# FFN down projection of a diffusion layer: two of the four weight sums of a chunk formed by accumulating transfers, the second output half carried negated

## The chip, the cores and the metric

The kernel runs on one core of one Trainium2 chip. The metric is the device time of one execution in microseconds (us). A core has TensorE (PE in the profile, its weight loads PEld), VectorE (DVE), ScalarE (ACT), GpSimd (POOL) and SyncE (SP), each with an instruction queue of its own that it works through in order, and 16 DMA engines that carry out the transfers these queues issue.

## What is computed

One layer of a hybrid model for 640 tokens (512 latent, 128 context) of 2048 channels: a modulated norm, one input projection, two groups of heads (gated DeltaNet and latent attention), an output projection with a gated residual, then a second modulated norm and a gated convolutional FFN, again with a gated residual, and a final norm. The change lies in the last product of the FFN:

```
def conv_ffn(h, w_up, conv_w, conv_b, w_down):
    u = depthwise_conv_centred(h @ w_up, conv_w) + conv_b
    a, gate = jnp.split(u, 2, axis=-1)
    return (jax.nn.silu(a) * gate) @ w_down

x = x + gate2 * conv_ffn(h2, w_up, ffn_conv_w, ffn_conv_b, w_down)
y = rms_norm(x, final_norm_g)
```

`w_down` is 5632 x 2048 in float32. Products are exact to near float32: each operand is split into a high and a low part, and three of the four part products are summed.

## The kernel before, in words

The tokens lie in the columns (640), the channels in the 128 partitions. Both FFN products are computed by halves of output channels, contraction and tokens, with 7 products in the place of 8 (Strassen's scheme in Winograd's form). For a pair of output tiles (256 channels) with weight quarters A11, A12 (first output half, first and second half of the contraction) and A21, A22 (second output half), the weights' side needs A11, A12, A22 and four sums:

```
S1 = A21 + A22     S2 = S1 - A11     S3 = A11 - A21     S4 = A12 - S2
```

**FFN down, order of the work.** The contraction is cut into 11 groups n, the output into 8 pairs p. A weight chunk (n, p) is 128 x 4 x 256, 512 KB: two contraction tiles of each half. `blocks`, `order` and `units` (lines 1478 to 1481) list the work: block 0 is four chunks by plain products (unit W); blocks 1 to 8 have eight chunks each (four pairs by two groups), block 9 twelve, block 10 eight. Each of these 84 chunks is two units: R (A11, S3, A12, A22; 24 matmuls of 128x128 by 320 columns) and S (S1, S4, S2; 18 matmuls).

**The loop** over the units (from line 1781) does, for unit u: `d_prep(u + 1)`, `d_mm(u)`, `d_post(u - 1)`, the residual of a finished pair, one step of the operands made ahead (`g_steps`).

- `d_load(i)` (L1524, DMA at L1527) loads chunk i on SP's queue into a `wraw` buffer, of which there are two; it is called for i + 2 when the R weights of chunk i have been split.
- `d_sums(i)` (L1529) forms the four sums on POOL: S1 at L1535 into a buffer `us` or `vs` (by the parity of i, one of each), the three differences by `sub` (its instruction stands at L1267); S3 takes the place of A21 inside `wraw`. It is called when the S weights of the chunk before have been split. Each is an instruction of 128 x 256.
- `d_prep(u)` splits the weights of a unit into `whi` by ACT (L922) and `wlo` by DVE (L923), two buffers of each; so it runs one unit ahead of the matmuls.
- `d_mm(u)` (L1594 high parts, L1597 low parts) accumulates in PSUM, tiles `mm` for R and `dn` for S.
- `d_post(u, q)` at a pair's last group adds the products to the output, which lies in SBUF (`xw`, `x_hi`, `x_lo`): ACT copies two products into `x` and `y` (L1622, L1623, one buffer of each), DVE adds what is read from PSUM, and POOL does three additions of 128 x 320 between SBUF tiles (L1601 is the helper `add` of both engines).
- `g_prep(j)` (L1512, instructions at L1517) makes the operands' sums: four subtractions of 128 x 320 on POOL for each of a group's two tiles, then splits by ACT and DVE.
- `residual2` (from line 1653), in the blocks 9 and 10: squares on ACT (L1666), added on POOL (L1668).

The program builder takes these instructions in the order in which they are written, but may move one ahead of another on the same engine where nothing depends on it. Waits between engines are put in by it.

Of the kernel before, what the change touches and what calls it, by code (L numbers as in the profile page):

```python
# [54 lines left out]
def _order():  # L55
    """the output tiles of the input projection"""
# [11 lines left out]
def step_kernel(ctx: ExitStack, tc: tile.TileContext, a, dbg=None, stop=None):  # L68
# [38 lines left out]
    # ------------------------------------------------------------ the stream of weight chunks  # L107
# [31 lines left out]
    def w_next():  # L139
        """the parts of the next chunk; the one after it is split and two more are loading."""  # L140
        i = pos[0]
        pos[0] += 1
        w_split(i)
        w_split(i + 1)
        w_load(i + 2)
        w_load(i + 3)
        raws_.pop(i, None)
        return parts.pop(i)

    # ------------------------------------------------------------ background work  # L150
# [7 lines left out]
    def fill_tick(n=1.0):  # L158
        """the filler advances by one unit every fill["step"] ticks."""
# [21 lines left out]
    # ------------------------------------------------------------ products  # L181
    def mm3(ps_list, wts, k, col, movs, start, stop):
        """ps += w^T m over the exact parts: hi.hi + hi.lo + lo.hi."""
# [9 lines left out]
    def hi_pass(outs, wts, col, mov, start, ticks=True):  # L193
        """outs = or += w_hi^T (m_hi + m_lo) over 4 k tiles."""
# [8 lines left out]
    def lo_pass(outs, wts, col, mov, stop, ticks=True):  # L203
        """outs += w_lo^T m_hi over 4 k tiles."""
# [13 lines left out]
    def dense(movs, sink, ntile=2, before=None, alloc=None, ext=0):  # L218
        """ntile output tiles, contraction over 16 tiles of 128."""
# [27 lines left out]
    # ------------------------------------------------------------ conditioning  # L247
# [9 lines left out]
    def ada(n, t0, cond, pl):  # L257
        """tiles t0 and t0 + 1 of the modulation; the last step is left to the caller"""
# [19 lines left out]
    def gain(t0, vg, n):  # L278
        """mod[scale] <- g * (1 + scale) for n channel tiles."""
# [4 lines left out]
    def modulated(x, rb, hi, lo, kt, scale, v):  # L284
        """(hi, lo) <- x * rb * gs; columns 0:512 by c, the rest by c_ctx."""
# [6 lines left out]
    def gemv_fill(pl, jobs):  # L292
        """vectors times matrices of up to 512 columns, in steps; a job: the weights of a k tile, the columns,
        the vectors [P, k, 2], and what becomes of the sums [P, (tile, c)]."""
# [47 lines left out]
    def ada_jobs(t0, t1):  # L342
        """four tiles of the modulation at a time"""
# [10 lines left out]
    # ------------------------------------------------------------ first norm, modulation, input projection  # L354
# [3 lines left out]
    # the normed and scaled tokens, and the two shifts as further columns  # L358
# [8 lines left out]
    with tc.tile_pool(name="xp", bufs=1, side="right") as xp:  # L367
# [25 lines left out]
        def early(i, ps):  # L393
            """z of a head, without the shift's part"""
# [45 lines left out]
    # ------------------------------------------------------------ gated DeltaNet  # L440
# [1472 lines left out]
```

## Time and profile before

| | us |
|---|---|
| median of 3 runs | 3420.69 (3416.08 to 3429.83) |
| span of the profiled execution | 3419.2 |
| PE busy in it | 3136.4 (92%) |
| DVE busy | 2657.2 (78%) |
| ACT busy | 1445.7 (42%) |
| POOL busy | 1584.5 (46%) |
| FFN down, from the first R unit's matmuls to the last S unit's | about 2778 to 3391 |

The span is that of one profiled execution, from the first instruction to the last; the median is that of the runs, 1.5 us more. The busy shares are averages over stages that differ: the slices of the page and the table by stretch show each stage by itself. In a group's row stand the line, the engine, the operation, what it writes and reads, the shape and the count; behind the bar the busy time, the mean of one in ns, and the idle time of the engine just before, with what ended it. Weight quarters and their sums have the names of their buffers: `wraw`, `us`, `vs`.

### The profile page before, as it was taken

How to read it: one execution, taken by the hardware profiler on the slowest of the kernel's cores; microseconds unless marked ns; L12 is line 12 of the kernel's file. 1: busy time of each engine (PE TensorE's matmuls, PEld its weight loads, DVE VectorE, ACT ScalarE, POOL GpSimd, SP SyncE). 2: the span in 40 equal slices, each digit the busy share in tenths (PEclk: the TensorE clock that was granted, in tenths of full speed). 3: DMA queues.
4: the chain of work that ended last, by engine and by line, in shares of the span. 5: the costliest groups of instructions: out<-in, count | busy, mean ns of one | idle time of the engine just before them, and what ended most of it. 6: DMA issues, size and time to landing. Idle time of an engine off the chain costs nothing.

```text
span 3419.2 us, 54842 instructions
## 1 busy us (share of the span) xinstructions
PE 3136.4 (92%) x21243; PEld 3017.4 (88%) x21243; DVE 2657.2 (78%) x3954; ACT 1445.7 (42%) x2230; POOL 1584.5 (46%) x1128
## 2 busy tenths in 40 slices
PE   5889999999999989997899999999999989988896
PEld 4689989889888979997799899999999988888895
DVE  7765666867576759998978887987888778787877
ACT  5434554554545542116344344344334444333433
POOL 1211111111100002326466566566566589999986
PEclk9998999998999999998899999999999999999998
DMA  7652222323242227772333433333332233232323
GB/s 268 215 169 64 81 81 72 102 67 97 65 140 73 78 69 274 268 240 86 123 102 98 126 109 101 117 104 102 119 109 95 97 118 101 88 99 90 104 99 116
DMA packets 181477, 403.94 MB, mean 118 GB/s; under 512 B 39392, under 2 KB 57952, under 8 KB 181216
## 3 DMA queue, kind: packets, MB, share of 16 engines
q1 hardware_dynamic: 181216, 400.44, 36.3%
q8 instruction: 167, 2.74, 0.3%
q14 instruction: 94, 0.77, 0.1%
HBM read 361.83 MB, written 38.54 MB: 117 GB/s over the span
## 4 chain that ended last, share of the span: by engine, by line
PE 55%; DVE 18%; POOL 11%; issue 6%; DMA 5%; ACT 4%; SPq 0%; DVEq 0%; POOLq 0%; ACTq 0%
PE mm L198 17%; PE mm L207 9%; PE dn L198 7%; DVE aacc L326 4%; PE dn L207 4%; DMA araw<-in_w_ada_dram 3%; PE mm L1594 3%; DVE wlo L923 2%; POOL wraw L1267 2%; PE pj L188 2%; DVE L L640 1%; DVE wlo L131 1%; PE mm L1083 1%; DVE tm L638 1%; POOL us L1267 1%
## 5 line engine op out<-in xcount | busy, mean ns | idle before, releaser
L131 POOL TENSOR_TENSOR wlo<-wraw,whi 128x1024 fp32r<-128x1024 f32 x61 | 189.6, 3109 | 986.6 <-PE mm L207 462.3
L923 DVE TENSOR_TENSOR wlo<-wraw,whi 128x1024 fp32r<-128x1024 f32 x256 | 402.5, 1572 | 162.5 <-ACT whi L922 82.8
L922 ACT CAST whi<-wraw 128x1024 fp32r<-128x1024 f32 x256 | 267.9, 1047 | 463.1 <-PE dn L198 159.7
L326 DVE SCALAR_TENSOR_TENSOR aacc<-araw,csil,aacc 128x512 f32<-128x512 f32 x510 | 421.1, 871 | 20.8 <-DMA araw<-in_w_ada_dram 19.8
L198 PE MATMUL mm<-b_hi,whi 128*128 128x320 f32 x1344 | 404.0, 314 | 11.3 <-ACT whi L922 10.5
L198 PE MATMUL mm<-b_lo,whi 128*128 128x320 f32 x1344 | 402.0, 313 | 0.0
L198 PE MATMUL mm<-h_hi,whi 128*128 128x320 f32 (+1 forms) x1312 | 330.5, 331 | 9.1 <-ACT h_hi L289 6.7
L198 PE MATMUL mm<-h_lo,whi 128*128 128x320 f32 (+1 forms) x1312 | 320.6, 324 | 12.3 <-POOL h_lo L290 12.3
L198 PE MATMUL dn<-b_hi,whi 128*128 128x320 f32 x1008 | 298.3, 310 | 1.0 <-ACT whi L922 1.0
L198 PE MATMUL dn<-b_lo,whi 128*128 128x320 f32 x1008 | 298.2, 309 | 0.0
L1594 PE MATMUL mm<-b_hi,whi 128*128 128x320 f32 x672 | 216.1, 335 | 67.6 <-DVE x_lo L1601 21.4
L198 PEld LDWEIGHTS mm<-b_hi,whi 128*128 128x128 f32 x1344 | 257.7, 192 | 13.4 <-ACT whi L922 12.3
L1294 POOL TENSOR_TENSOR us<-wraw,wraw 128x512 f32<-128x512 f32 x83 | 138.9, 1674 | 275.8 <-DVE wlo L923 275.8
L207 PE MATMUL mm<-b_hi,wlo 128*128 128x320 f32 x1344 | 234.2, 318 | 27.6 <-DVE wlo L923 27.5
L129 ACT CAST whi<-wraw 128x1024 fp32r<-128x1024 f32 (+1 forms) x138 | 142.8, 1035 | 273.9 <-PE mm L198 189.1
L198 PEld LDWEIGHTS mm<-b_lo,whi 128*128 128x128 f32 x1344 | 257.2, 191 | 0.0
L1267 POOL TENSOR_TENSOR wraw<-wraw 128x512 f32<-128x512 f32 (+1 forms) x168 | 247.6, 1474 | 13.1
L198 PEld LDWEIGHTS mm<-h_lo,whi 128*128 128x128 f32 x1312 | 230.9, 197 | 16.1 <-POOL h_lo L290 14.2
L198 PEld LDWEIGHTS mm<-h_hi,whi 128*128 128x128 f32 x1312 | 230.1, 198 | 15.1 <-ACT h_hi L289 8.7
L207 PEld LDWEIGHTS mm<-b_hi,wlo 128*128 128x128 f32 x1344 | 210.2, 194 | 31.8 <-DVE wlo L923 31.2
L207 PE MATMUL mm<-h_hi,wlo 128*128 128x320 f32 (+1 forms) x1312 | 235.9, 321 | 0.0
L1594 PE MATMUL mm<-b_lo,whi 128*128 128x320 f32 x672 | 212.2, 330 | 0.0
(533 smaller groups left out, 8436.8 us busy)
## 6 DMA issues: line engine op xcount, KB each, us to landing
wraw<-in_w_up_dram SPq DMA_DIRECT2D x176, 512.0 KB
araw<-in_w_ada_dram SPq DMA_DIRECT2D x272, 256.0 KB
wraw<-in_w_down_dram SPq DMA_DIRECT2D x88, 512.0 KB
wraw<-in_w_in_dram SPq DMA_DIRECT2D x80, 512.0 KB
araw<-in_w_ada_dram SPq DMA_DIRECT2D x56, 512.0 KB
wraw<-in_w_out_dram SPq DMA_DIRECT2D x32, 512.0 KB
graw<-g_d SPq DMA_DIRECT2D x44, 320.0 KB
g_d<-cg SPq DMA_DIRECT2D x44, 256.0 KB
```

Of the source, the lines that this page charges most:

```text
L129: act.copy(hi[:, :, 0:n], raw[:, :, 0:n])
L131: (pool if on_pool else dve).tensor_tensor(lo[:, :, 0:n], raw[:, :, 0:n], hi.bitcast(F32)[:, :, 0:n], ALU.subtract)
L188: pe.matmul(out, w[:, k, col:col + P], m[:, sl], start=start and n == 0, stop=stop and n == 2)
L198: pe.matmul(o, wts[0][:, k, col:col + P], m[:, sl], start=start and k + n == 0, stop=False)
L207: pe.matmul(o, wts[1][:, k, col:col + P], mov(k)[0][:, sl], start=False, stop=stop and k == 3)
L326: dve.scalar_tensor_tensor(acc[:, c, 0:w], raw, vecs[:, kt, c:c + 1], acc[:, c, 0:w], ALU.mult, ALU.add)
L638: dve.tensor_tensor(tv, L[:, j + 1:32, j:j + 1].broadcast_to([40, n, j]), L[:, j, 0:j].unsqueeze(1).broadcast_to([40, n, j]), ALU.mult)
L922: act.copy(dst_hi, src)
L923: dve.tensor_tensor(dst_lo, src, dst_hi.bitcast(F32), ALU.subtract)
L1267: pool.tensor_tensor(out, x, y, ALU.subtract)
L1294: pool.tensor_tensor(s1, a21, a22, ALU.add)
L1594: pe.matmul(dq[q], wt(w[0], k), bs[(2 * n + k) % 6][m][:, q, :], start=n == grp[0] and k + m == 0, stop=False)
```

## The change

Two of the four sums per chunk are no longer computed by POOL instructions. The weights are laid out anew before the launch: a chunk's four slots of 256 columns are now A12, A11, A22 and A21. The buffer of a chunk is loaded with A12, A11, A22 and, in the fourth slot, A11 once more; `s_load` loads A22 into the first third of the S buffer. Then `d_accum` issues two transfers from POOL's queue that read A21 from memory and add it to what lies in SBUF: A11 + A21 in the fourth slot, A22 + A21 in the S buffer. An accumulating transfer can add but not subtract, so the second output half is carried negated: with A21 and A22 taken as negative, A11 + A21 is S3, A22 + A21 is -S1, A11 - S1 is -S2 and A12 - S2 is S4. `d_sums` keeps two additions on POOL. The signs in `d_post` follow, and each add stays on its engine; at the end c22 and c21 have the right sign again. `s_load(i + 2)` is called where the S weights of chunk i are split, `d_accum(i + 1)` at the end of the loop's step before the R unit of chunk i. Comments and docstrings of the whole file are gone as well, which is left out here.

```diff
+    def d_src(i):
+        return a["w_down"][order[i][2], order[i][1]]
+
     def d_load(i):
         if i < len(order):
-            draw[i] = wp.tile([P, 4, 256], F32, tag="wraw", name="wraw")
-            sp.dma_start(draw[i], a["w_down"][order[i][2], order[i][1]])
+            draw[i] = r = wp.tile([P, 4, 256], F32, tag="wraw", name="wraw")
+            if order[i][0] == 0:
+                sp.dma_start(r, d_src(i))
+            else:
+                sp.dma_start(r[:, 0:3], d_src(i)[:, 0:3])
+                sp.dma_start(r[:, 3], d_src(i)[:, 1])
+
+    def s_load(i):
+        if i < len(order) and order[i][0] > 0:
+            ws[i] = wy.tile([P, 4, 256], F32, name=("us", "vs")[i % 2])[:, 0:3]
+            sp.dma_start(ws[i][:, 0], d_src(i)[:, 2])
+
+    def d_accum(i):
+        if i < len(order) and order[i][0] > 0:
+            pool.dma_start(draw[i][:, 3], d_src(i)[:, 3], accum_op=ALU.add)
+            pool.dma_start(ws[i][:, 0], d_src(i)[:, 3], accum_op=ALU.add)

     def d_sums(i):
         if i < len(order) and order[i][0] > 0:
-            r = draw[i]
-            a11, a21, a12, a22 = r[:, 0:2, 0:P], r[:, 0:2, P:256], r[:, 2:4, 0:P], r[:, 2:4, P:256]
-            s = wy.tile([P, 4, 256], F32, name=("us", "vs")[i % 2]).rearrange("p n (k c) -> p n k c", k=2)[:, 0:3]
-            ws[i] = s
-            pool.tensor_tensor(s[:, 0], a21, a22, ALU.add)
-            sub(a21, a11, a21)
-            sub(s[:, 2], s[:, 0], a11)
-            sub(s[:, 1], a12, s[:, 2])
+            r, s = draw[i], ws[i]
+            pool.tensor_tensor(s[:, 2], s[:, 0], r[:, 1], ALU.add)
+            pool.tensor_tensor(s[:, 1], r[:, 0], s[:, 2], ALU.add)
...
         if c == "S":
...
+            split(hi[:, 0:3], lo[:, 0:3], ws.pop(i))
         else:
-            split(hi, lo, draw.pop(i))
+            split(hi, lo, draw[i])
             d_load(i + 2)
         if c != "R":
+            s_load(i + 2)
+            if c == "W":
+                d_accum(i + 1)
             d_sums(i + 1)
+            draw.pop(i)
         return hi, lo
...
             if new:
                 add(dve, c11, x, q[Q2])
-                add(dve, c21, y, q[Q4], ALU.subtract)
+                dve.scalar_tensor_tensor(c21, y, -1.0, q[Q4], ALU.mult, ALU.subtract)
...
-        add(dve, x, x, q[Q6])
+        add(dve, x, x, q[Q6], ALU.subtract)
...
             add(dve, y, y, x)
-            add(dve, c12, c12, q[Q5])
+            add(dve, c12, c12, q[Q5], ALU.subtract)
             add(dve, c12, c12, q[Q3])
             add(dve, c22, c22, q[Q5])
             add(pool, c12, c12, x)
-            add(pool, c21, c21, y)
-            add(pool, c22, c22, y)
+            add(pool, c21, c21, y, ALU.subtract)
+            add(pool, c22, c22, y, ALU.subtract)
...
         for _ in range({0: 5, 9: 2}.get(b, 1)):
             next(prep, None)
+        if u + 1 < len(units) and units[u + 1][1] == "R":
+            d_accum(units[u + 1][0] + 1)
...
-    out["w_down"] = pairs(i["w_down"][0]).transpose(1, 0, 2, 3, 4)
+    w = pairs(i["w_down"][0]).transpose(1, 0, 2, 3, 4).reshape(11, 8, P, 2, 2, 2, P)
+    out["w_down"] = np.stack([w[:, :, :, h, :, j] for j, h in ((0, 1), (0, 0), (1, 1), (1, 0))], 3).reshape(11, 8, P, 4, 256)
```

In `d_mm` and `plain` the weights are picked from the new slots; the matmuls and their order are the same.

## Rows read from the trace of the kernel before

**Rows 1.** The page's slices: busy tenths of POOL in 40 equal slices of the span.

```profile
POOL 1211111111100002326466566566566589999986
```

**Rows 2.** Table by stretch: us; PE, PEld, DVE, ACT, POOL busy (instructions); clock, DMA share, GB/s.

```profile
2778.00:2890.00 112.00, 104.22 (x672) 102.48 (x672) 84.48 (x98) 46.79 (x68) 103.60 (x96) 0.96 0.32 99
2890.00:3185.60 295.60, 263.85 (x1680) 258.92 (x1680) 237.85 (x281) 112.26 (x160) 284.92 (x261) 0.95 0.29 94
...
3246.00:3328.00 82.00, 78.06 (x504) 76.19 (x504) 58.60 (x70) 28.58 (x38) 67.45 (x63) 0.97 0.31 103
```

**Rows 3.** The chain that ended last: start, us, piece; 16 matmuls, nothing between.

```profile
2691.75 2.35 PE dn L198 x16
```

**Rows 4.** Groups by line and form, 2890 to 3185.6: idle time of PE and ACT.

```profile
L1594 PE MATMUL mm<-b_hi,whi 128*128 128x320 f32 x320 | 103.5, 337 | 31.7 <-DVE x_lo L1601 12.3 <-DVE xw L1601 11.0 <-DVE x_hi L1601 8.2
...
L922 ACT CAST whi<-wraw 128x1024 fp32r<-128x1024 f32 x40 | 42.0, 1051 | 133.3 <-PE mm L1594 81.6 <-POOL wraw L1267 38.6 <-DVE xw L1601 8.0
...
L1623 ACT COPY y<-mm 128x320 f32<-128x320 f32 x20 | 8.6, 430 | 10.0 <-POOL x_hi L1601 5.9 <-POOL x_lo L1601 3.9
```

**Rows 5.** The chain up to a restart of PE: start, us, piece.

```profile
3031.05 1.43 POOL us L1535
...
3034.82 1.81 POOL x_hi L1601
...
3036.65 0.43 ACT y L1623
...
3037.51 0.49 DVE x_lo L1601
...
3038.14 1.87 PE mm L1594 x10
```

**Rows 6.** Groups by line and form, POOL, 2890 to 3185.6.

```profile
L1267 POOL TENSOR_TENSOR wraw<-wraw 128x256 f32<-128x256 f32 x40 | 47.5, 1187 | 3.1
L1601 POOL TENSOR_TENSOR x_lo<-x_lo,y 128x320 f32<-128x320 f32 x22 | 26.1, 1186 | 1.3 <-DVE y L1601 1.3
...
L1535 POOL TENSOR_TENSOR us<-wraw 128x256 f32<-128x256 f32 x20 | 21.3, 1064 | 0.0
L1267 POOL TENSOR_TENSOR vs<-vs,wraw 128x256 f32<-128x256 f32 x20 | 21.1, 1057 | 0.0
...
L1535 POOL TENSOR_TENSOR vs<-wraw 128x256 f32<-128x256 f32 x20 | 19.1, 953 | 2.3 <-DVE x_lo L1601 1.6 <-DMA wraw<-in_w_down_dram 0.7
...
L1517 POOL TENSOR_TENSOR graw<-graw 128x320 f32<-128x320 f32 x10 | 13.4, 1343 | 0.8
```

**Rows 7.** Instructions of line L1527: duration in ns, least, median, most.

```profile
L1527 SPq DMA_DIRECT2D wraw<-in_w_down_dram x88: 327/328/376, 2710.7 to 3371.6; - x88
```

**Rows 8.** POOL in order of time, from 2970: start, us, instruction.

```profile
2970.56 1.86 POOL L1601 TENSOR_TENSOR x_lo<-x_lo,y 128x320 f32<-128x320 f32 x1
2972.38 1.45 POOL L1535 TENSOR_TENSOR us<-wraw 128x256 f32<-128x256 f32 x1
2973.91 0.74 POOL L1267 TENSOR_TENSOR wraw<-wraw 128x256 f32<-128x256 f32 x1
2974.61 0.88 POOL L1601 TENSOR_TENSOR x_hi<-x_hi,x 128x320 f32<-128x320 f32 x1
2975.45 0.74 POOL L1267 TENSOR_TENSOR us<-us,wraw 128x256 f32<-128x256 f32 x1
```

**Rows 9.** POOL's waits, 2778 to 3390: for whom, us in total, times, longest.

```profile
POOL vs L1535 <- DMA wraw<-in_w_down_dram: 4.0, 4, 2.0
...
POOL us L1535 <- DMA wraw<-in_w_down_dram: 3.0, 2, 2.0
```

**Rows 10.** The chain: waits for a landing (80 KB, 320 KB, 512 KB).

```profile
721.75 3.33 DMA Lc<-l_d
...
2724.67 3.00 DMA graw<-g_d
...
3234.99 3.47 DMA wraw<-in_w_down_dram
```

**Rows 11.** SP's waits, 2850 to 3200: for whom, us in total, times, longest.

```profile
SPq L1527 <- DVE wlo L923: 278.6, 49, 8.1
```

**Rows 12.** Groups by line and form, 2890 to 3185.6: the split of S weights.

```profile
L922 ACT CAST whi<-vs 128x768 fp32r<-128x768 f32 x20 | 16.7, 836 | 22.8 <-PE dn L1594 19.3 <-DVE wlo L923 2.0 <-POOL vs L1267 1.4
...
L923 DVE TENSOR_TENSOR wlo<-vs,whi 128x768 fp32r<-128x768 f32 x20 | 29.1, 1456 | 7.7 <-ACT whi L922 7.7
```

More of the change, by code (lines that the diff above doesn't have):

```diff
@@ L1547, in d_prep @@
         if c == "S":
-            h, l = (t.rearrange("p k c -> p (k c)")[:, 0:768] for t in (hi, lo))
-            split(h, l, ws.pop(i).rearrange("p n k c -> p (n k c)"))
-            hi, lo = (t.rearrange("p n (k c) -> p n k c", k=2) for t in (hi, lo))
+            split(hi[:, 0:3], lo[:, 0:3], ws.pop(i))
         else:
-            split(hi, lo, draw.pop(i))
+            split(hi, lo, draw[i])
             d_load(i + 2)
         if c != "R":
+            s_load(i + 2)
+            if c == "W":
+                d_accum(i + 1)
             d_sums(i + 1)
+            draw.pop(i)
         return hi, lo
@@ L1570, in plain @@
                     for (o, _), x in zip(tok_chunks(ps[i]), mov(k, m)):
-                        pe.matmul(o, w[part][:, k, i * P:i * P + P], x, start=n + k == 0, stop=n == 2 and k == 3)
+                        pe.matmul(o, w[part][:, ((1, 3), (0, 2))[k // 2][i], k % 2 * P:k % 2 * P + P], x,
+                                  start=n + k == 0, stop=n == 2 and k == 3)
         return ps
@@ L1586, in d_mm @@
         if c == "R":
-            jobs = [(q, lambda h, k, r=r, c=c: h[:, r + k, c:c + P]) for q, r, c in
-                    ((Q2, 2, 0), (Q1, 0, 0), (Q4, 2, P), (Q7, 0, P))]
-        else:
-            jobs = [(q, lambda h, k, m=m: h[:, m, k, :]) for m, q in ((2, Q6), (0, Q5), (1, Q3))]
+            js = ((0, Q2), (1, Q1), (2, Q4), (3, Q7))
+        else:
+            js = ((2, Q6), (0, Q5), (1, Q3))
+        jobs = [(q, lambda h, k, m=m: h[:, m, k * P:k * P + P]) for m, q in js]
         for q, wt in jobs:
@@ L1632, in d_post @@
         x, y = dt.pop(p)
-        add(dve, x, x, q[Q6])
+        add(dve, x, x, q[Q6], ALU.subtract)
         if new:
-            add(dve, c12, x, q[Q5])
+            add(dve, c12, x, q[Q5], ALU.subtract)
             add(pool, y, x, y)
             add(dve, c12, c12, q[Q3])
-            add(pool, c21, c21, x)
-            add(dve, c22, y, q[Q5])
+            add(pool, c21, c21, x, ALU.subtract)
+            add(dve, c22, q[Q5], y, ALU.subtract)
         else:
             add(dve, y, y, x)
-            add(dve, c12, c12, q[Q5])
+            add(dve, c12, c12, q[Q5], ALU.subtract)
             add(dve, c12, c12, q[Q3])
@@ L1705, in step_kernel @@
             d_load(1)
-            d_sums(0)
             w2 = d_prep(0)
```

## The prediction

> **What bounds the kernel now.** I read the slices of the page first, to see where engines change roles. In the last fifth, the FFN down stage, GpSimd (POOL) stands at 8 to 9 tenths where it stood at 4 to 6 in the stage before [rows 1]. Then the table by stretch: in the 295.6 us from 2890 (blocks 3 to 7 of the stage, 40 weight chunks) POOL is busy 284.9 us, 96%, and a chunk takes 295.6 / 40 = 7.39 us; the ninth block is looser [rows 2]. Next the pace that TensorE (PE) would keep alone: 16 matmuls in a row take 2.35 us, 0.147 us each; a chunk has 24 (unit R) + 18 (unit S) = 42, the 1680 of the stretch over 40, so 6.17 us [rows 2, 3]. So 1.22 us a chunk are lost, and the idle time of the engines says to whom: PE's 31.7 us end with VectorE's (DVE's) reads of PSUM, and ScalarE's (ACT's) copies into x and y ahead of these wait until POOL has finished with the last x and y; ACT's split of the R weights waits for POOL too, 38.6 us, for the difference that POOL writes among them [rows 4]. The chain closes the loop: up to 3036.6 it is POOL, instruction after instruction, then ACT's copy of y, then DVE, then PE [rows 5]. So POOL's queue bounds this stage, by its length and not by one late instruction. The stage has 84 chunks with sums, from 2778 to 3393: 615 us, against 84 x 6.17 = 518 us at PE's pace. Nothing that relieves POOL can bring more than 97 us.
>
> **The sum, part by part.** *Removed from POOL*, per chunk: A21 + A22 and A11 - A21. In blocks 3 to 7 these are the groups of 47.5, 21.3 and 19.1 us, 87.9 us for 80 instructions: 2.20 us a chunk, 1.10 each [rows 6]. What stays on POOL is (284.9 - 87.9) / 40 = 4.93 us a chunk: two sums of 1.06 us or so, three additions to the output of 1.1 to 1.2 us for every second chunk, eight subtractions of about 1.3 us for the operands in every eighth [rows 6].
>
> *Added to POOL*, per chunk: two issues of accumulating transfers. No transfer is issued by POOL before, so the issue is bounded by neighbours: SyncE (SP) issues one of 512 KB in 0.33 us; the slowest additions that POOL does here take 1.86 us [rows 7, 8]. A POOL issue is work of this engine over 128 rows, so I place it nearest to its ordinary instruction of 128 rows, 1.10 us. Then two issues cost 2.20 us and cancel what is removed: 4.93 + 2.20 = 7.13 busy us, as now. By the ends it is 5.59 or 8.65.
>
> *A wait that POOL did not have.* Before, POOL waited for weights a handful of times in the whole stage, 7 us in all [rows 9]. Afterwards the first remaining sum reads S1, which the second accumulating transfer of the same chunk completes; in program order the two sums come directly behind the two issues, with nothing of POOL's in between. A wait there holds up the output additions queued behind it, which is the very work that PE waits for. How long: rows of landing give 3.00 us for 320 KB, 3.33 us for 80 KB, 3.47 us for 512 KB, so size hardly matters; this one is of 128 KB, and I take 3.0 [rows 10]. Low end 3.0, high end 6.9, twice the longest, since it also reads what it adds to.
>
> How much of the 3.0 us is covered? The builder does not keep program order on POOL: output additions stand between the sums of one chunk where those wait on each other [rows 8]. In a block there are 8 waits, 24 us. Four of them can be filled by the output additions (some 3.4 us at the end of each pair), two by the operands' subtractions (two lumps of four, 5 us each); two have nothing. So between 2 of 8 (well ordered) and 8 of 8 (as written) stay open: 0.75 to 3.0 us a chunk. I take a third, 1.0 us, since the builder demonstrably mixes but the fillers also have inputs of their own: 84 x 1.0 = 84 us. The looser stretches at both ends take some of it: POOL idles 8.4 us in the first two blocks and 14.5 us in the ninth [rows 2], of which I count two thirds, 15 us. Net: 84 - 15 = **+69 us**.
>
> The Trainium skill ("DMA: Bandwidth & Descriptors", Latency and other measured facts; Anatomy of one DMA) has two figures for a transfer issued from GpSimd, about 1 us to its first byte and 2.0 us plus the bytes over 436 GB/s to its end, which makes an estimate of 2.3 us here; no run shown has such a transfer. By these the same sum would be 84 x (2.0 - 2.2 + 0.77) - 15 = +33 us, 3454.
>
> *Other edits.* SP goes from one issue a chunk to three, 0.33 us each; it spends its time waiting for splits [rows 11], and the new load of S1 waits for a split too (that of the chunk two earlier, whose buffer it takes); behind it stand only loads for later chunks and operands, so this costs nothing while those 278.6 us of waiting in 350 are there; if that cover were gone, each late load would show as POOL waiting to issue. The ring of two S buffers closes in time: split 0.84 + 1.46, load 0.33 + 3.0, issue 1.1, landing 3.0, two sums 2.1: 11.8 us of the 12.3 that two chunks take at PE's pace [rows 10, 12]. That is close: at that pace any queueing would show, at today's 14.8 there are 3 us to spare. Traffic rises from 512 KB to 896 KB a chunk plus the read-back; at 0.29 of the engines' time [rows 2] that fits, at about half. The R split waits for its accumulated slot in place of POOL's difference; that is issued one chunk (6.2 us) ahead against 1.1 + 3.0 us: nothing. Flipped signs replace additions by subtractions of the same shape and engine; four of block 1 become a scalar_tensor_tensor. Nothing. The new weight layout is made before the launch; the first four chunks, plain products, only pick other columns.
>
> The profile's span is 3419.2 us, 1.5 us under the median of the three runs, 3420.7. 3420.7 + 69 gives **3490 us**.
>
> **Rivals.** *Relief (faster).* POOL's sums are stretched by VectorE: the same 256 columns take 0.74 us or 1.45 and more, depending on what runs beside [rows 8]. VectorE's splits around it subtract two operands of SBUF. An issue reads no tile through the engine; if it therefore costs the unstretched 0.74, a chunk saves 2.20 - 1.48 = 0.72 us, 84 x 0.72 = 60 us, and if the waits are covered as well the time is 3360. This decides where 2 issues plus open wait stay below 2.20 us. With 0.33 it would run into PE's 6.17: 3324. The rule is the Trainium skill's ("SBUF — State Buffer", Who interferes with whom): a VectorE instruction with two SBUF inputs excludes a GpSimd instruction that reads SBUF, not one that only writes. The two durations agree with it, and it speaks for this rival; that the issue counts as a writer no row shows. For it: POOL is 96% busy, so any relief is paid out at once. Against it: the wait, which lands on the same queue.
>
> *Waits in program order (much slower).* All 8 waits open: 84 x 3.0 - 15 = +237, 3658. For it: sums and issues are neighbours in the code. Against: the mixing in [rows 8].
>
> *No change.* Issues at 1.10 and fillers for all waits but those that today's idle time takes: within 17 us of 3421. The engine would be as full as now, with other work. This is also what comes of it if the change does not take the work off POOL but only renames it: each addition is still started on its queue.
>
> **How the numbers follow.** The forecast (a third to two thirds of the waits open) gets 0.40, program order 0.14, no change 0.13, relief 0.33. The range 3345 to 3600 holds relief except for its extreme, and the forecast up to two thirds of the waits open (3420.7 + 84 x 2.0 + 11 us for issues a little dearer); all waits open and issues at 1.86 us lie above it. The slower cases alone would be 3438 to 3600. A measurement here tells about 0.5%, 17 us. Slower 0.54, same 0.13, faster 0.33.
>
> **What the new profile would show.** Right: two POOL issues a chunk near 1.1 us; POOL waiting for a landing before its first sum, in sum some 80 us; PE idle longer before the same lines; a block of eight chunks at 66 to 68 us rather than 59. Wrong: issues well under 0.8 us with POOL under 90% busy and PE near 6.2 us a chunk (relief); POOL waiting to issue rather than to add (the load of S1 late); or SP or ACT as the one that PE waits for, which the sum has at nothing.

## The result, and the profile after

The changed kernel takes 3548.55 us (median of 4 runs, 3546.80 to 3553.54) beside 3420.66 us for the kernel before: a ratio of 1.0376, 95% interval [1.0356, 1.0397], 128 us slower. The profiled execution has a span of 3547.4 us. In the listing of the changed kernel, S3's transfer (into `wraw`) is issued at L1548 and S1's (into `us` or `vs`) at L1549; the two sums that stay on GpSimd (POOL) are L1554 and L1555, the output additions L1621, and the matmuls L1614 and L1617. The loads stand at L1536, L1537 and L1543.

First the page's slices, which answer to [rows 1]: busy tenths of POOL and of the DMA engines.

```profile
POOL 1221111111010014344665665665665676667554
DMA  7742223223241267733333333333323545555554
```

In most slices of the last fifth POOL has gone from 8 and 9 tenths to 5 to 7, and the kernel is slower all the same. The engine that was full is not full any more: what bounds the stage now is something that POOL stands still for. The table by stretch, over the windows of [rows 2], says the same in numbers (columns as there).

```profile
2778.00:2890.00 112.00, 92.94 (x563) 90.53 (x562) 61.40 (x80) 34.81 (x49) 68.38 (x76) 0.92 0.50 118
2890.00:3185.60 295.60, 242.04 (x1395) 232.15 (x1395) 201.67 (x232) 92.31 (x135) 197.98 (x211) 0.88 0.50 121
...
3246.00:3328.00 82.00, 66.37 (x391) 63.47 (x392) 55.77 (x67) 26.34 (x40) 55.12 (x58) 0.90 0.50 119
```

In the same 295.6 us TensorE (PE) does 1395 matmuls in place of 1680, so a chunk of 42 takes 295.6 x 42 / 1395 = 8.90 us, where it took 7.39. POOL is busy 198.0 us of them (it was 284.9), VectorE (DVE) 201.7 (237.9). Everything is idler, and the DMA engines' share has gone from 0.29 to 0.50. Of the 1.51 us by which a chunk is longer, 0.82 are idle time of PE and 0.69 are slower matmuls: a matmul has 0.174 us of PE's busy time where it had 0.157, at a mean granted clock of 0.88 of the upper level, 2.4 GHz, where it was 0.95, with more idle time ahead of the R unit's first matmuls (43.4 us in this stretch, it was 31.7). That the clock sets the time is not shown: in the chain that ended last between 2890 and 3400, the transfers into `vs` and `us` have 27.3% and 17.6%, more than any line of an engine. An idle engine on a slower path waits; the groups by line and form of that stretch name the wait (the POOL lines answer to [rows 6], the ACT line to [rows 4], the DVE line to [rows 12]).

```profile
L1548 POOL DMA_DIRECT2D wraw<-in_w_down_dram x32 | 27.8, 870 | 0.0
...
L1549 POOL DMA_DIRECT2D us<-in_w_down_dram x16 | 18.9, 1184 | 0.0
L1549 POOL DMA_DIRECT2D vs<-in_w_down_dram x16 | 17.7, 1108 | 0.0
L1554 POOL TENSOR_TENSOR us<-us,wraw 128x256 f32<-128x256 f32 x16 | 14.9, 934 | 33.1 <-DMA us<-in_w_down_dram 33.1
L1554 POOL TENSOR_TENSOR vs<-vs,wraw 128x256 f32<-128x256 f32 x17 | 13.9, 815 | 61.1 <-DMA vs<-in_w_down_dram 61.1
...
L922 ACT CAST whi<-wraw 128x1024 fp32r<-128x1024 f32 x33 | 34.6, 1048 | 129.9 <-DMA wraw<-in_w_down_dram 99.8 <-PE dn L1617 11.4 <-DVE b_lo L923 7.1
...
L923 DVE TENSOR_TENSOR wlo<-vs,whi 128x768 fp32r<-128x768 f32 x16 | 44.1, 2758 | 22.1 <-ACT whi L922 19.8 <-PE mm L1614 2.3
```

Three things are new here. The sum that reads S1 finds POOL idle for 33.1 + 61.1 us ahead of it, always for the landing of the accumulating transfer. ScalarE's (ACT's) split of the R weights, which waited for PE and for POOL's difference, now waits 99.8 us for a transfer into `wraw`. And one of DVE's splits has gone from a mean of 1456 ns to 2758. Over the whole stage, POOL's waits (to be laid beside the 7 us of [rows 9]) are:

```profile
POOL vs L1554 <- DMA vs<-in_w_down_dram: 149.8, 40, 5.5
POOL us L1554 <- DMA us<-in_w_down_dram: 100.4, 35, 5.3
```

That is 250.2 us, 2.98 us for each of 84 chunks, in 75 of them. And ACT's, over the same time:

```profile
ACT whi L922 <- DMA wraw<-in_w_down_dram: 169.0, 42, 5.5
```

The instructions of the two issuing lines, with who waited and how long the transfers took to land:

```profile
L1548 POOL DMA_DIRECT2D wraw<-in_w_down_dram x84: 848/871/889, 2748.5 to 3503.7; - x84
...
  ACT whi L922: 153.4, 38
...
DMA to landing us min/median/max: 3.1/4.4/6.3
...
L1549 POOL DMA_DIRECT2D vs<-in_w_down_dram x42: 866/1184/1193, 2717.9 to 3504.3; - x42
...
DMA to landing us min/median/max: 3.1/4.1/6.7
```

In order of time, POOL and then one line of DVE, one finds all three again (start, us, instruction; in brackets the idle time ahead of it):

```profile
3007.34 0.87 POOL L1548 DMA_DIRECT2D wraw<-in_w_down_dram  x1
3007.95 1.17 POOL L1621 TENSOR_TENSOR x_hi<-x_hi,x 128x320 f32<-128x320 f32 x1
3008.79 1.16 POOL L1621 TENSOR_TENSOR x_lo<-x_lo,y 128x320 f32<-128x320 f32 x1
3009.61 1.18 POOL L1549 DMA_DIRECT2D us<-in_w_down_dram  x1
3013.20 1.35 POOL L1554 TENSOR_TENSOR us<-us,wraw 128x256 f32<-128x256 f32 x1 [2.41 <-DMA us<-in_w_down_dram]
3014.62 0.73 POOL L1555 TENSOR_TENSOR us<-wraw,us 128x256 f32<-128x256 f32 x1
3015.29 0.87 POOL L1548 DMA_DIRECT2D wraw<-in_w_down_dram  x1
3015.87 1.19 POOL L1549 DMA_DIRECT2D vs<-in_w_down_dram  x1
3022.54 1.16 POOL L1554 TENSOR_TENSOR vs<-vs,wraw 128x256 f32<-128x256 f32 x1 [5.48 <-DMA vs<-in_w_down_dram]
...
3007.45 3.32 DVE L923 TENSOR_TENSOR wlo<-vs,whi 128x768 fp32r<-128x768 f32 x1 [1.50 <-ACT whi L922]
```

The output additions that POOL has (3007.95, 3008.79) are done ahead of the second issue, not behind it; behind it stands the sum that reads its result. Where no addition is at hand, the two issues stand back to back (3015.29, 3015.87) and POOL waits 5.48 us. An issue is shown with 0.87 to 1.19 us, but the next instruction starts 0.58 to 0.61 us after it. And the split that starts beside the additions behind an issue ends only after they are through (3007.45 to 3010.77, the additions to 3009.95).

### The profile page after: what moved, and what is told of

It is laid out like the page before. It is cut to its first block, busy times and chain, and to the rows that moved or that the text cites. A ratio compares the mean times of both kernels' runs of the same rounds, so it can differ in the third digit from the quotient of the medians.

```text
span 3547.4 us, 55448 instructions
## 1 busy us (share of the span) xinstructions
PE 3180.1 (90%) x21243; PEld 3050.4 (86%) x21243; DVE 2643.8 (75%) x3954; ACT 1443.5 (41%) x2230; POOL 1514.8 (43%) x1128
## 4 chain that ended last, share of the span: by engine, by line
PE 44%; DVE 17%; DMA 14%; POOL 11%; issue 7%; ACT 4%; SPq 0%; POOLq 0%; DVEq 0%; ACTq 0%
PE mm L198 15%; PE mm L207 8%; PE dn L198 7%; DMA vs<-in_w_down_dram 5%; DVE aacc L326 5%; DMA us<-in_w_down_dram 4%; PE dn L207 3%; DMA araw<-in_w_ada_dram 3%; DVE wlo L923 2%; PE pj L188 2%; DVE L L640 1%; POOL wraw L1548 1%; PE mm L1083 1%; DVE tm L638 1%; POOL x_lo L1621 1%
## 5 line engine op out<-in xcount | busy, mean ns | idle before, releaser
L131 POOL TENSOR_TENSOR wlo<-wraw,whi 128x1024 fp32r<-128x1024 f32 x61 | 199.2, 3266 | 979.4 <-PE mm L207 411.9
L923 DVE TENSOR_TENSOR wlo<-wraw,whi 128x1024 fp32r<-128x1024 f32 x256 | 385.1, 1504 | 234.7 <-ACT whi L922 139.4
L198 PE MATMUL mm<-b_hi,whi 128*128 128x320 f32 x1344 | 403.7, 314 | 11.3 <-ACT whi L922 10.6
L198 PE MATMUL mm<-b_lo,whi 128*128 128x320 f32 x1344 | 401.7, 312 | 0.0
L1614 PE MATMUL mm<-b_hi,whi 128*128 128x320 f32 x672 | 239.3, 367 | 106.5 <-DVE x_lo L1621 43.9
L198 PEld LDWEIGHTS mm<-b_hi,whi 128*128 128x128 f32 x1344 | 257.5, 192 | 13.4 <-ACT whi L922 12.4
L1614 PEld LDWEIGHTS mm<-b_hi,whi 128*128 128x128 f32 x672 | 154.6, 230 | 119.9 <-issue 74.3
L198 PEld LDWEIGHTS mm<-h_lo,whi 128*128 128x128 f32 x1312 | 230.8, 197 | 16.9 <-POOL h_lo L290 15.1
L1614 PE MATMUL mm<-b_lo,whi 128*128 128x320 f32 x672 | 231.6, 356 | 0.0
```

What stands on the lines that cost most here:

```text
L131: (pool if on_pool else dve).tensor_tensor(lo[:, :, 0:n], raw[:, :, 0:n], hi.bitcast(F32)[:, :, 0:n], ALU.subtract)
L198: pe.matmul(o, wts[0][:, k, col:col + P], m[:, sl], start=start and k + n == 0, stop=False)
L923: dve.tensor_tensor(dst_lo, src, dst_hi.bitcast(F32), ALU.subtract)
L1614: pe.matmul(dq[q], wt(w[0], k), bs[(2 * n + k) % 6][m][:, q, :], start=n == grp[0] and k + m == 0, stop=False)
```

## The experiments

All kernels are the changed one with the edit given, or, where the heading names another run, that one with the edit given. Quarters 0 to 3 of a chunk in memory are A12, A11, A22 and A21, so the loads and transfers can be read off the indices; `...` marks lines left out. Lines with - are taken out, lines with + put in.

### What the layout costs, and what the two sums are worth

**e3: four sums on POOL.** The changed layout and signs, each chunk in one load, no transfers from POOL.

```
-                sp.dma_start(r[:, 0:3], d_src(i)[:, 0:3])
-                sp.dma_start(r[:, 3], d_src(i)[:, 1])
+            sp.dma_start(r, d_src(i))
...
-            sp.dma_start(ws[i][:, 0], d_src(i)[:, 2])
...
-            pool.dma_start(draw[i][:, 3], d_src(i)[:, 3], accum_op=ALU.add)
-            pool.dma_start(ws[i][:, 0], d_src(i)[:, 3], accum_op=ALU.add)
...
+            pool.tensor_tensor(s[:, 0], r[:, 3], r[:, 2], ALU.add)
+            pool.tensor_tensor(r[:, 3], r[:, 3], r[:, 1], ALU.add)
             pool.tensor_tensor(s[:, 2], s[:, 0], r[:, 1], ALU.add)
```

> The new weight layout and the negated half stay, but no accumulating transfer and no load of S1's start: GpSimd forms all four sums again, as additions. If the 128 us come from the transfers (their landing, their issue or their traffic), this is the kernel before within 0.5%: 3405 to 3437 us. If they come from the layout, the signs or the split loads, it stays above 3480.

Measured: 3421.12 us, ratio 1.0002 [0.9988, 1.0017]. Layout and signs cost nothing.

**e4: no transfers at all.** Both issues are left out; S1 and S3 are then incomplete (A22 and A11 alone).

```
-            pool.dma_start(draw[i][:, 3], d_src(i)[:, 3], accum_op=ALU.add)
-            pool.dma_start(ws[i][:, 0], d_src(i)[:, 3], accum_op=ALU.add)
```

> Leaves the accumulating transfers out: A21 is never added, two of the four sums are missing from the output; the three plain loads a chunk and the two additions on GpSimd stay. It shows what the rest of the change is worth. Theories wait and issue: GpSimd has 4.9 us a chunk, TensorE sets the pace at 6.17, so 84 x 1.2 = 97 us under before at most: 3320 to 3345. If the split loads or their order on SyncE cost something of their own, it stays above 3380.

Measured: 3344.16 us (one run), some 76 us under the kernel before. The table by stretch, e3 first, then e4:

```profile
2900.00:3160.00 260.00, 235.26 (x1496) 231.00 (x1495) 206.83 (x245) 96.30 (x137) 248.69 (x230) 0.95 0.29 93
```

```profile
2900.00:3160.00 260.00, 251.88 (x1683) 246.67 (x1682) 214.57 (x282) 112.26 (x160) 202.04 (x180) 1.00 0.41 127
```

With two sums taken off POOL and nothing in their place, PE is busy 251.9 of 260 us and a chunk takes 260 x 42 / 1683 = 6.49 us. So the reading of the kernel before was right: POOL's queue was the bound, and its relief is paid out at once, up to some 76 us. With less idle time PE has a granted clock of 1.00, and 0.150 us a matmul. SyncE's (SP's) three loads a chunk are all in e4, so what they cost lies inside the 21 us that e4 stays short of the 97; the whole loss is in the two transfers from POOL, which spend those 76 us and 128 more.

### The two transfers, one at a time, and each a chunk earlier

**e1: S3 alone by transfer**, S1 a POOL addition.

```
-            sp.dma_start(ws[i][:, 0], d_src(i)[:, 2])
+            sp.dma_start(ws[i][:, 0], d_src(i)[:, 3])
-            pool.dma_start(ws[i][:, 0], d_src(i)[:, 3], accum_op=ALU.add)
+            pool.tensor_tensor(s[:, 0], s[:, 0], r[:, 2], ALU.add)
```

> Only S3 (the fourth slot of the R weights) is formed by a transfer; S1 is an addition on GpSimd again, from a plain load. GpSimd then waits for no accumulating transfer before its sums. Theory wait (GpSimd's queue stands still for the landing of S1's transfer just ahead of the sums): GpSimd's work falls from 7.13 to 4.93 + 1.10 + 0.6 = 6.6 us a chunk and nothing stops it, so faster than before by some 84 x 0.5 = 40 us, 3360 to 3400. Theory load (what costs is that R weights are complete later: load, then landing of 4.4 us): it keeps most of the loss, 3480 to 3540. Theory issue (the issue itself is dear on GpSimd): half the loss, about 3485.

Measured: 3427.99 us, ratio 1.0023 [1.0012, 1.0034], outside the ranges of all three theories. POOL is relieved (226.7 of 260 us busy), and nothing comes of it. ACT's waits between 2778 and 3360 say why:

```profile
ACT whi L922 <- PE mm L1614: 99.6, 28, 8.3
ACT whi L922 <- DMA wraw<-in_w_down_dram: 99.4, 21, 6.9
```

The R weights come late. They have a loop of their own: there are two `wraw` buffers, and the load of chunk i + 2 may start when DVE has split chunk i; then follow the load, the place of L1548 in POOL's queue, its landing, and the split of chunk i + 2. By the rows that is 1.05 + 1.36 us of split, about 3.5 of load [rows 10], 0.6 of issue and 4.4 of landing, 10.9 us, against 12.3 us for two chunks at PE's pace, and each wait in POOL's queue ahead of the issue is added to it. With e1's own landing (3.2 in the median) and DVE split (2.18) it is 10.5. So the sum by itself closes in time; what it leaves out are the waits in the queues, and POOL stands 63 us at L1548 alone in that stretch. The sum is an estimate, but the chain that ended last between 2900 and 3160 agrees: 16.9% of it is the transfer into `wraw` and 13.4% the DVE split.

**e2: S1 alone by transfer**, S3 a POOL addition (the reverse of e1); each chunk in one load, as in e3.

```
-            pool.dma_start(draw[i][:, 3], d_src(i)[:, 3], accum_op=ALU.add)
+            pool.tensor_tensor(r[:, 3], r[:, 3], r[:, 1], ALU.add)
             pool.tensor_tensor(s[:, 2], s[:, 0], r[:, 1], ALU.add)
```

> S1 alone is formed by a transfer, issued where the change issues it; S3 is a GpSimd addition again, so the R slot has no accumulating transfer. GpSimd per chunk by the rows: 7.39 - 1.10 + 0.6 of issue = 6.9 us. The wait theory (GpSimd stands for the landing of the S accumulate directly ahead of the sums that read it): the S3 addition lies in front of that wait and hides 0.9 us of it, some 2 us stay open, so GpSimd needs about 8.9 us a chunk and the run comes out at 3480 to 3530. The theory that only the late R weights cost time (their buffer's loop of load, issue, landing, split): with nothing in the R slot this run is at 3380 to 3400, faster than the kernel before.

Measured: 3512.49 us, ratio 1.0260 [1.0242, 1.0277]: the wait theory's 3480 to 3530. POOL's waits between 2778 and 3360:

```profile
POOL vs L1550 <- DMA vs<-in_w_down_dram: 104.5, 33, 4.5
POOL us L1550 <- DMA us<-in_w_down_dram: 73.7, 28, 4.7
```

**e5: both by transfer, S1's a chunk earlier**, into the quarter of the S buffers that no part uses, so that a buffer serves two chunks in turn.

```
+    def s_slot(i):
+        return 0 if i // 2 % 2 else 3
...
-            sp.dma_start(ws[i][:, 0], d_src(i)[:, 2])
+            sp.dma_start(ws[i][:, s_slot(i)], d_src(i)[:, 2])
...
-            pool.dma_start(ws[i][:, 0], d_src(i)[:, 3], accum_op=ALU.add)
+    def s_accum(i):
+            pool.dma_start(ws[i][:, s_slot(i)], d_src(i)[:, 3], accum_op=ALU.add)
...
-            s_load(i + 2)
+            s_load(i + 3)
             if c == "W":
                 d_accum(i + 1)
+                s_accum(i + 2)
```

> Both transfers stay, but S1's is issued a chunk earlier: the unused fourth quarter of each S buffer takes the S1 of the chunk after next. Theory wait: the 250 us of GpSimd's waits go, GpSimd has 4.93 + 1.2 = 6.1 us a chunk, at TensorE's pace of 6.17, so well under before: 3340 to 3390. Theory load: ScalarE's 169 us of waits for the R weights stay and with them the time, 3480 to 3550. Theory issue: no change against the changed kernel, 3548.

Measured: 3454.92 us, ratio 1.0103 [1.0083, 1.0123], between the ranges of the theories. Of the 128 us, 94 are back. POOL no longer waits for the S transfer; what is left between 2778 and 3360 is the R buffer, in POOL and in ACT:

```profile
POOL vs L1564 <- DMA wraw<-in_w_down_dram: 70.6, 18, 5.2
```

```profile
ACT whi L922 <- DMA wraw<-in_w_down_dram: 182.8, 35, 8.6
```

**e8: S1 alone by transfer, a chunk earlier** (e5's edit, with e2's).

```
-            pool.dma_start(draw[i][:, 3], d_src(i)[:, 3], accum_op=ALU.add)
+            pool.tensor_tensor(r[:, 3], r[:, 3], r[:, 1], ALU.add)
```

> As the run with S1 alone by transfer, but the transfer is issued a chunk earlier, into the quarter of the S buffer that is unused, so that it has landed when the sums come to it. If the two waits found so far (GpSimd for the S landing, ScalarE's split for the R landing) are all that the change costs, both are gone here, GpSimd has 7.39 - 1.10 + 0.6 = 6.9 us a chunk, 0.5 less than before on 84 chunks = 41 us, and the run is at 3375 to 3395. If what the earlier-issue run had left over (3455) came from the earlier issue itself, or from accumulating transfers whatever they write, this is at 3420 to 3460.

Measured: 3417.36 us, ratio 0.9989 [0.9976, 1.0003]. The two waits are gone and with them the loss, but the time is in neither range: the 3375 to 3395 are not reached, and the 3420 to 3460 just missed. The four kernels make a square:

| | S1's transfer in its own chunk | a chunk earlier | what that saves |
|---|---|---|---|
| S3 by transfer | 3548.6 (the change) | 3454.9 (e5) | 94 |
| S3 by POOL | 3512.5 (e2) | 3417.4 (e8) | 95 |
| what that saves | 36 | 38 | |

Each part saves the same whether the other is there or not, so the loss has two causes that add up here (94 + 38 or 36 + 95 of the 131 us between the change and e8): POOL standing for S1's landing, and S3's transfer, which makes the R weights late. The 36 to 38 us are what that transfer costs on balance, against a POOL addition, and only where S1 goes by transfer. With S1 on POOL the same swap costs 7 us (e1 beside e3); most likely because POOL is then the bound, and the addition taken off it pays for most of the delay.

### Why relief then brings nothing

**e9: e1 with the R slot's transfer sent elsewhere**, plain, into a quarter of the S buffer that nobody reads; S3 is left out (slot 3 keeps A11; the expectation says A12). `ws4[i]` is the whole S buffer of chunk i.

```
-            pool.dma_start(draw[i][:, 3], d_src(i)[:, 3], accum_op=ALU.add)
+            pool.dma_start(ws4[i][:, 3], d_src(i)[:, 3])
```

> The run in which S3 alone went by transfer (3428, no gain although GpSimd was busy 22 of 260 us less), with one edit: the transfer into the R buffer's slot 3 goes, plain, to a quarter of an S buffer that nobody reads, and slot 3 keeps the plain A12, so one sum is left out. GpSimd issues as many transfers and the same bytes move, only nobody waits for the landing. If the R weights' buffer loop held that run (split, load into the freed buffer, issue, landing, split), it falls to 3370 to 3395. If GpSimd's issue or the transfers themselves held it, it stays at 3420 to 3430.

Measured: 3398.86 us, ratio 0.9926 [0.9909, 0.9943], 29 us under e1 and 4 us short of the range of the buffer theory. The edit changes the kind of transfer too, and the square takes the issue away together with the wait, so neither separates the two by itself. What speaks for the buffer is the chain, 2900 to 3160: the transfer into `wraw`, 16.9% in e1, has no place in e9's, the DVE split has 1.5% (it was 13.4%), and PE's matmuls make 83%.

**e10: e9's copy issued by SP.**

```
-            pool.dma_start(ws4[i][:, 3], d_src(i)[:, 3])
+            sp.dma_start(ws4[i][:, 3], d_src(i)[:, 3])
```

> The run whose third-slot transfer went, plain, to a quarter that nobody reads (3399; one sum left out), with that transfer issued from SyncE instead of GpSimd. Nothing else differs. Theory of the blocked split: behind a transfer issued from GpSimd its additions run through back to back (a start each 0.7 to 0.84 us) and VectorE's split that starts beside them is held until the run ends (3.3 to 6.5 us in the runs with such transfers, at most 1.9 in the kernel before); with no transfer on GpSimd the longest split is back under 2.4 us, its mean in the stretch 2900 to 3160 falls from 2065 to some 1500 ns, and the run comes to 3350 to 3375. Theory that only GpSimd's own time counts: 0.56 us of issue less per chunk on an engine that was busy 235 of 260 us, splits as long as they were, 3385 to 3399.

Measured: 3382.33 us, ratio 0.9887 [0.9864, 0.9910]: 16.5 us less, between the two ranges in time, but in the length of the splits as the theory of the held split has it. The DVE split of the R weights and the table by stretch, e9:

```profile
L923 DVE TENSOR_TENSOR wlo<-wraw,whi 128x1024 fp32r<-128x1024 f32 x37 | 76.4, 2065 | 3.6 <-ACT whi L922 2.0 <-issue 1.5
```

```profile
2900.00:3160.00 260.00, 242.40 (x1557) 236.49 (x1557) 227.62 (x252) 100.79 (x143) 234.99 (x241) 0.96 0.42 131
```

and e10:

```profile
L923 DVE TENSOR_TENSOR wlo<-wraw,whi 128x1024 fp32r<-128x1024 f32 x38 | 57.6, 1517 | 1.4 <-ACT whi L922 1.4
```

```profile
2900.00:3160.00 260.00, 249.01 (x1612) 242.40 (x1611) 217.25 (x266) 108.75 (x157) 232.43 (x209) 0.97 0.45 139
```

The mean goes from 2065 to 1517 ns (1522 in the kernel before) with POOL as busy as it was (235.0 and 232.4 us). So it is not POOL's load that stretches the splits, but that POOL issues transfers and runs on behind them (in e2, where it stands still behind its issue, the mean is 1321). Whether the 16.5 us come from the splits is not shown: the edit also takes off POOL the issue itself (0.56 us) and the 19 us, between 2778 and 3360, in which POOL stood at that issue for DVE. e8 shows how far it goes, in POOL's order of time and one line of DVE:

```profile
2981.70 0.87 POOL L1550 DMA_DIRECT2D vs<-in_w_down_dram  x1
2982.31 1.18 POOL L1630 TENSOR_TENSOR x_lo<-x_lo,y 128x320 f32<-128x320 f32 x1
2983.15 1.03 POOL L1560 TENSOR_TENSOR wraw<-wraw 128x256 f32<-128x256 f32 x1
2983.84 1.03 POOL L1561 TENSOR_TENSOR us<-us,wraw 128x256 f32<-128x256 f32 x1
2984.54 1.15 POOL L1630 TENSOR_TENSOR x_lo<-x_lo,x 128x320 f32<-128x320 f32 x1
...
2986.89 1.15 POOL L1550 DMA_DIRECT2D us<-in_w_down_dram  x1
...
2981.84 6.45 DVE L923 TENSOR_TENSOR wlo<-wraw,whi 128x1024 fp32r<-128x1024 f32 x1 [0.18 <-ACT whi L922]
```

Behind the issue the additions start 0.69 to 0.84 us apart, as fast as POOL's shortest ones of [rows 8], and the split that began beside them lasts until they are over, 6.45 us. Of the 36 splits of R weights between 2900 and 3160, nine take over 2.4 us. In the kernel before, where POOL was 96% busy, no such split took over 1.92 us: the two engines took turns, and each was stretched a little. It is the likeliest reason that e8 has no gain (POOL is busy 223 of 260 us there, and DVE 221, up from 207); in e8 it was not taken away by itself, only in e10. The trace of e8 also shows where a late split comes back to POOL:

```profile
POOL wraw L1560 <- DMA wraw<-in_w_down_dram: 45.5, 19, 6.0
```

Between 2778 and 3360 the first sum waits for the plain load of the R weights, 7 us in the kernel before. That load can start only when DVE's split has freed the buffer, so the loop of the `wraw` buffers has a part in e8 as well; how much of the missing gain it is, no run separates.

**e11: e8 with the transfer issued just ahead of the three sums**, whose first waits for the R weights.

```
     def d_sums(i):
+        s_accum(i + 1)
...
-                s_accum(i + 2)
```

> The run with S1 alone by transfer and a chunk early (3417), with the transfer issued straight ahead of the chunk's three sums, not between sums and posts. If the held splits are what keeps that run from its 3385, and what follows the issue decides how long they are held, then an issue whose next addition waits for the R weights leaves a gap for VectorE: splits of 1.5 to 2 us, 3385 to 3405. If they are held as long as before, 3410 to 3425.

Measured: 3419.32 us, ratio 1.0004 [0.9991, 1.0016], the second alternative: the splits are held longer than in e8, where the mean of this row is 2254 ns.

```profile
L923 DVE TENSOR_TENSOR wlo<-wraw,whi 128x1024 fp32r<-128x1024 f32 x36 | 96.2, 2673 | 7.2 <-ACT whi L922 6.9 <-issue 0.2
```

### The price of an issue, and of adding

**e12: e3 with one accumulating transfer a chunk that nobody reads.**

```
+            sp.dma_start(ws4[i][:, 3], d_src(i)[:, 2])
...
+            pool.dma_start(ws4[i][:, 3], d_src(i)[:, 3], accum_op=ALU.add)
```

> The run with all four sums on GpSimd (3421), with one accumulating transfer per chunk added, from GpSimd, into a quarter of the S buffers that nobody reads: the price of an issue by itself, with no wait for its landing. By the prediction's 1.10 us an issue: 84 times 1.10 = 92, so 3500 to 3515. By the start-to-start time of 0.6 us behind an issue in the changed kernel's trace: 84 times 0.6 = 50, so 3460 to 3475. If the additions run faster behind an issue, as its trace shows (0.7 to 0.84 us apart), and that gives the issue back: 3420 to 3440.

Measured: 3452.99 us, ratio 1.0105 [1.0088, 1.0122]; 31.9 us over e3, 0.38 us an issue (with the plain load from SP that goes ahead of it). That is below both prices that were put forward (1.10 and 0.6) and above nothing. The rows behind it are the issues, the landings and the stretch:

```profile
L1547 POOL DMA_DIRECT2D vs<-in_w_down_dram x42: 853/872/1013, 2717.9 to 3413.1; - x42
...
DMA to landing us min/median/max: 3.1/3.2/7.4
```

```profile
2900.00:3160.00 260.00, 222.73 (x1387) 214.89 (x1387) 227.92 (x229) 93.27 (x132) 255.54 (x245) 0.93 0.45 121
```

POOL is at 255.5 of 260 us. It takes 0.6 us for an issue and gets some of it back, most likely by the additions that run through behind it, which was not taken apart further; DVE pays, with 227.9 us for 229 instructions, where e3 has 206.8 for 245.

**e7: the change with plain copies for accumulating transfers** (both sums are left out).

```
-            pool.dma_start(draw[i][:, 3], d_src(i)[:, 3], accum_op=ALU.add)
-            pool.dma_start(ws[i][:, 0], d_src(i)[:, 3], accum_op=ALU.add)
+            pool.dma_start(draw[i][:, 3], d_src(i)[:, 3])
+            pool.dma_start(ws[i][:, 0], d_src(i)[:, 3])
```

> The changed kernel with both GpSimd transfers as plain copies instead of accumulating ones: the two sums are left out, the issues, the places and the waits are the same. If the adding makes the landing long (4.1 and 4.4 us median now, against 3.0 to 3.5 us for the plain loads of the rows), landings fall to about 3 us and the run to 3440 to 3480. If a transfer that GpSimd issues lands in about 4 us whatever it does, the run stays at 3530 to 3550.

Measured: 3491.69 us (one run), between the two ranges. The issue and the landing of the S copies:

```profile
L1549 POOL DMA_DIRECT2D vs<-in_w_down_dram x41: 536/538/556, 2792.3 to 3448.1; - x41
DMA to landing us min/median/max: 2.5/3.1/5.9
```

A plain copy is issued in 0.54 us where an accumulating one takes 0.87 to 1.18, and lands in 2.5 us at best and 3.1 in the median, where that took 3.1 and 4.1. So the adding accounts for some 57 of the 128 us, and a plain copy in that place costs the other 71: POOL still waits 216 us for the S copies, where it waited 250.

### Another way to relieve POOL

**e13: e3 with S3 on DVE**, ahead of the R split; no transfers from POOL, and S1 and the other two sums stay on it.

```
-            pool.tensor_tensor(r[:, 3], r[:, 3], r[:, 1], ALU.add)
...
+            if c == "R":
+                dve.tensor_tensor(draw[i][:, 3], draw[i][:, 3], draw[i][:, 1], ALU.add)
             split(hi, lo, draw[i])
```

> No transfers: the run with four sums on GpSimd (3421) with S3, the one that the R split itself needs, moved to VectorE directly ahead of that split, everything computed. GpSimd loses 1.10 of 7.39 us per chunk and gets no issue; VectorE gains a 128x256 addition of some 0.4 to 0.5 us per chunk (by its 128x320 rows of 479 ns) on 207 of 260 us busy. If GpSimd's queue was the bound and a transfer from it was the wrong way to relieve it, this is as fast as the run with the transfer on SyncE plus VectorE's added time at most: 3375 to 3405, faster than both kernels. If the kernel is bound by the two engines together (they hold each other up in additions), the moved sum gives nothing: 3415 to 3425.

Measured: 3448.23 us, ratio 1.0087 [1.0072, 1.0102], a miss of both. S3 overwrites A21, which POOL still has to read for S1; so the addition, 426 ns by itself, holds DVE's whole queue until POOL has got there. DVE's waits in the stretch of 260 us:

```profile
DVE wraw L1564 <- POOL vs L1549: 38.7, 13, 4.2
...
DVE wraw L1564 <- POOL us L1549: 6.9, 13, 0.6
```

It is the change's own fault in another place: work moved off a full queue, to where its operand is late. No complete version among these beats the kernel before; e8 and e11 only equal it.

## Why the prediction was right, and where it was not

*The bound, and what its relief is worth*: right. POOL's queue set the stage, and nothing could bring more than 97 us; without the two sums, 76 come (e4), and then PE is the bound.

*Slower, by a wait on the queue whose relief was sought*: right, and this mechanism carries the larger part, 94 of the 128 us. The time, 3549, is in the range, 59 us above the forecast of 3490. Two terms of the sum were mis-sized and one step was wrong. That the time is no further off is in part luck: the two terms erred in opposite directions, the issues by 84 us too many (84 x 2 x 0.5) and the open wait by 166 us too few (84 x 1.98).

*Two issues at 1.10 us each*: too dear. An issue is shown with 0.87 to 1.18 us, but delays the next instruction by 0.58 to 0.61; by itself it costs 0.38 us a chunk (e12). The low end, taken from SP, was nearer than the neighbour on POOL that I chose.

*The wait, 3.0 us of which two thirds are covered*: the landing took 4.1 us in the median, within the bounds of 3.0 and 6.9, and the cover is what failed. I let a third of the waits stay open, 1.0 us a chunk; open are 2.98 us, in 75 chunks of 84. The output additions do stand among the transfers, but ahead of the second issue, as the order of time shows, so that nothing of them is left for the wait. That is the rival "program order" for the wait, with cheaper issues: with both sizes put right the sum gives 84 x (2 x 0.60 - 2.20 + 2.98) - 15 = +151, not far from the +128 measured; this does not confirm the sum, since the late R weights are not in it.

*The R split, "issued one chunk ahead: nothing"*: the step that failed. I compared the issue and the landing with the chunk between, and not with the loop that they lengthen: a `wraw` buffer is free only after a split, then loaded, then added to, and only then split again. ACT waits 169 us in all for `wraw`; undoing this part saves 36 to 38 us where S1 goes by transfer (the square), and 7 where it does not (e1). A loop was reckoned for the S buffers, at 11.8 of 12.3 us, and none for these.

*Other edits at nothing*: layout and signs cost nothing, as forecast (e3); SP's loads cost 21 us at most (e4). What the sum does not have at all is the held split of DVE; what it costs in the change itself, no run separates. The rival "relief" drew on the rule for the very pair of engines, and took the other side of it: that POOL would be faster beside DVE's splits. It is (0.69 to 0.84 us behind an issue), and the split beside it is held.

The Trainium skill ("SBUF — State Buffer", Who interferes with whom) says that a VectorE instruction with two SBUF inputs contends with GpSimd instructions that read SBUF, and that the order of issue decides who is held. That the two contend agrees with the held split of 6.45 us beside POOL's run of additions. The order does not, as the rows of e8 stand: the split starts at 2981.84 and the first addition at 2982.31, and it is the split that is held; why a transfer issued by POOL turns the order round, no run here shows. The Trainium skill ("DMA: Bandwidth & Descriptors", Anatomy of one DMA) has 2.0 us plus the bytes over 436 GB/s, an estimate of 2.3 us for this transfer: the plain copy comes near at its best (2.5), the accumulating one does not (3.1 at best, 4.1 to 4.4 in the median here), and the measurement decides.

The marks that I named for the new profile came out mixed. POOL does wait ahead of its first sum, 250 us and not 80; a block takes 8 x 8.90 = 71 us and not 66 to 68; the issues are shown with 0.87 and some 1.1 to 1.2 us, near the mark, but hold up the next instruction by 0.6 only. POOL under 90% busy, which I gave as a mark of relief, is here the mark of the wait: a queue that waits for its own transfers is idle too, and the busy share by itself says nothing of the sign.

## What to carry to other kernels

Work that is moved from an engine to a transfer leaves a landing in its place; it can pay only if the reader of the result comes later than the landing, on a queue that has other work behind the issue and ahead of that reader, and in e8 and e11 even that brought no gain. Reckon for every buffer that the transfer writes the whole loop (freed, loaded, issued, landed, read, freed again), not only the one that looks tight. And count what an issue on GpSimd does to VectorE's instructions beside it, not only what it takes of GpSimd.

## What the runs showed of the hardware

- An accumulating transfer of 128 KB issued from GpSimd lands in 3.1 us at best, whichever kernel it is in; a plain one in 2.5 (e7, e9). The issue is shown with 0.87 to 1.18 us in the median (0.83 at least) against 0.54 to 0.56. The median landing is 3.2 to 3.6 us with one such transfer a chunk (e1, e2, e8, e12) and with the two of e5, and 4.1 to 4.4 in the change, where S1's takes 3.5 us into `us` and 5.1 into `vs`; what makes the difference, no run here separates.
- Additions on GpSimd that follow a transfer it issued can run through, starting 0.69 to 0.84 us apart, without letting in a VectorE split that begins beside them: a split of 1.2 us alone, at most 1.92 beside additions without transfers from GpSimd, was held for up to 6.46 us in e8 and 7.56 in e12.
